# One level of Strassen in the down projection of a two-layer feed-forward, with weight splitting shared between two engines

## The chip, the core and the metric

The kernel runs on one core of a Trainium2 chip. Its engines each have their own instruction queue: TensorE (PE in the profile; its weight loads are PEld), VectorE (DVE), ScalarE (ACT), GpSimd (POOL) and SyncE (SP, which here issues DMA). The metric is the time of one execution in device microseconds (us), the median of several runs. All tensors are float32. The matmuls work on "fp32r" operands: a float32 number is split into a high part (a cast) and a low part (the number minus its high part), and a product is three matmuls, high x high, high x low and low x high, accumulated in PSUM.

## What is computed

A trunk of two layers on 512 tokens of width 1024: a recurrent mixer (layer 0) and stick-breaking attention (layer 1), each followed by a SwiGLU feed-forward of width 2816. The change lies in the feed-forward, whose reference is, per layer,

```
h = _rmsnorm(x, norm_ffn_g[layer])
x = x + (silu(h @ w_gate) * (h @ w_up)) @ w_down
```

with x 512 x 1024, w_gate and w_up 1024 x 2816 and w_down 2816 x 1024.

## The kernel before, in words

**Order of stages.** `run` (L1102) does the recurrent mixer, feed-forward 0, attention, feed-forward 1. The residual x is kept transposed in SBUF as eight tiles of 128 features x 512 tokens (`self.x`, L286).

**Units.** `ffn` (L611) walks over the 2816 hidden columns in six units (u = 0 to 5): five of 512 columns and a last one of 256. The gate and up products of a unit are already one 2 x 2 Strassen-Winograd step with seven products instead of eight (`product(q, ...)`, L632, q = 1 to 7). The stationary operands of these products are sums and differences of activations, prepared once per layer in `ffn_in` (L331); the moving operands are weight combinations. One product of a full unit is two chunks of 12 matmuls, 512 columns wide; of the last unit, one chunk of 24 matmuls, 256 wide. The products are collected in three pairs of PSUM banks that rotate from unit to unit (L679). `gate1` (L691) and the end of product 4 (L733 to L738) apply silu and the multiplication; the result is token-major, in the tiles `u2` and `hx`.

**Down.** The down projection of unit u-1 is woven into unit u. `turn` (L646) transposes two of the four 128-column blocks at a time on TensorE into banks 6 and 7 and splits them into high and low parts (`hh`). `down_pair` (L670) takes one weight chunk and makes two of the eight output tiles: 4 k tiles x 3 matmuls of 512 columns each, weights stationary, then one DVE add from PSUM onto x (L668). Four such pairs complete a full unit. Behind the loop (L741 to L782) follow the last pair or two of unit 4 and the half unit 5, into banks held open.

**Order.** In `ffn`, TensorE's instructions stay in program order (`manual_schedule`, L614); the other engines are ordered by a scheduler with priorities.

**Weights.** `plan` (L155) lists all weight chunks (128 x 1024, 512 KB) in order of use: 99 per feed-forward layer. `chunk` (L254) loads up to eight chunks ahead through SP's queue, and splits up to three ahead in the feed-forward: `Piece.source` (L74) first makes a Strassen combination on DVE where the product needs one (L76, 128 x 1024), then `split_piece` (L235) casts the high part on ACT (L236) and subtracts for the low part (L237) on the engine that `wl_engine` (L247) names. In a feed-forward the low parts of gate/up weights go to DVE and those of down weights to POOL. Outside, odd-numbered chunks go to POOL and even ones to DVE, except where listed. Four pairs of tiles take the split weights (three in one pool, `wh4`/`wl4` beside it, L223); with them the cast of a chunk waits until the matmuls four chunks back are done. Raw weights that are used once have four buffers (`raw_buf`), two quarters of each gate/up block have their own, doubled (`b1`, `b3`), and the running combination has two (`tt`).

**Norm.** For each x tile a square is added into `acc`, in `ffn_in` on POOL (L366, L380). In u = 0, between products 3 and 7, `norm_rs1` (L394) turns that into the tokens' scale with small matmuls and a chain of small DVE and ACT operations (L385 to L390).

**Slots.** Most 128 x 512 tiles come from an arena of 43 slots that lives throughout (NS1, x among them), and a second of 30 that exists only in the mixers (NS2).

Of the kernel before, what the change touches and what calls it, by code (L numbers as in the profile page):

```python
# [16 lines left out]
P = 128  # L17
# [12 lines left out]
NS1 = 43  # L30
NS2 = 30
FB = 512
NU = 5
# [11 lines left out]
class Unit:  # L45
    def __init__(self, kern, l, u):
        self.kern, self.u = kern, u
        self.w = FB if u < NU else FB // 2
        self.np = 2 if u < NU else 1
        self.kt = 2 if u < NU else 4  # L50
        self.src = kern.a["w_gu"][l, 8 * u:8 * u + 4 * self.np]
        self.b = {}


class Piece:
# [18 lines left out]
    def source(self):  # L74
# [20 lines left out]
        return b("t")  # L95


class Kern:
# [56 lines left out]
    def plan(self):  # L155
# [13 lines left out]
        def ffn(l):  # L169
            down = a["w_dn"][l]  # L170
            r = [self.unit(l, 0)]
            for u in range(1, NU + 1):
                p = self.unit(l, u)
                d = [[down[4 * (u - 1) + i]] for i in range(4)]
                h = len(p) // 7
                if u == 1:
                    order = (0, 1, 2, 3, d[0], 4, d[1], 5, d[2], 6, d[3])
                elif u < NU:
                    order = (0, 1, d[0], 2, 3, d[1], 4, d[2], 5, 6, d[3])
                else:  # L180
                    order = (0, 1, d[0], 2, 3, d[1], 4, 5, 6, d[2], d[3])
                r.append([e for q in order for e in (q if isinstance(q, list) else p[q * h:q * h + h])])
            r.append([down[20], down[21]])
            return [e for u in r for e in u]
# [17 lines left out]
    def unit(self, l, u):  # L202
        k = Unit(self, l, u)
        return [Piece(k, q, c) for q in ((1, 5, 6, 3, 7, 2, 4) if u else (1, 2, 5, 6, 3, 7, 4)) for c in range(k.np)]
# [78 lines left out]
    def setup(self):  # L283
        nc, a = self.nc, self.a
        c = self.const
        self.x = [self.new(f"x{k}") for k in range(KT)]  # L286
# [324 lines left out]
    def ffn(self, l, gnext):  # L611
        nc, tc = self.nc, self.tc
        mm = nc.tensor.matmul
        with tc.tile_pool(name=f"ffn{l}", bufs=1) as self.fp, tc.manual_schedule(engines={mybir.EngineType.PE}):  # L614
# [8 lines left out]
            tb = self.bank[6:]  # L623
            ab = [self.bank[2 * i:2 * i + 2] for i in range(3)]
# [3 lines left out]
            hh = [None] * 4  # L628
            hx = [self.new("hx", first=True) for _ in range(2)]
            rs = lambda t: self.rsT[:, t:t + 1]  # L630

            def product(q, unit, out, half, first=True):  # L632
# [13 lines left out]
            def turn(fs, banks, dst=None):  # L646
                for f, b in zip(fs, banks):
                    for t in range(NT):
                        nc.tensor.transpose(b[:, ts(t)], (u2 + hx)[t][:, ts(f)], self.ident)
                    h, lw = dst[f] if dst else (self.fp.tile([P, S], F32R, tag=f"{n}{f}", bufs=1,  # L650
                                                             name=f"{n}{f}_{self.used}") for n in ("hh", "hl"))
                    nc.scalar.copy(h, b)
                    nc.vector.tensor_tensor(lw, b, h.bitcast(F32), ALU.subtract)
                    if not dst:
                        hh[f] = (h, lw)

            def down(w, o, n, bank, first=True, last=True, cs=slice(0, S)):
                for k in range(n):
                    h, lw = hh[k]
                    ws = ts(o * n + k)  # L660
                    st, en = first and k == 0, last and k == n - 1
                    out = bank[:, :cs.stop - cs.start]
                    mm(out, lhsT=w[0][:, ws], rhs=h[:, cs], start=st, stop=False, skip_group_check=True)  # L663
                    mm(out, lhsT=w[0][:, ws], rhs=lw[:, cs], start=False, stop=False, skip_group_check=True)  # L664
                    mm(out, lhsT=w[1][:, ws], rhs=h[:, cs], start=False, stop=en, skip_group_check=True)  # L665

            def add(m, bank):
                nc.vector.tensor_tensor(self.x[m], self.x[m], bank, ALU.add)  # L668

            def down_pair(d):  # L670
                w = self.chunk()
                for i in range(2):
                    down(w, i, 4, tb[i])
                    add(2 * d + i, tb[i])

            for u in range(NU + 1):
                un = self.unit_of()
                w = un.w
                A, B, D = (ab[(u + i + l) % 3] for i in range(3))  # L679
                if u > 1:  # L680
                    turn((0, 1), tb)
                product(1, un, A, 0)
                for j in range(2):
                    nc.scalar.copy(r1[j][:, :w], A[j][:, :w])

                def second():
                    product(2, un, D, 0)
# [9 lines left out]
                if u == 0:  # L697
                    second()
                elif u > 1:
                    turn((2, 3), tb)  # L700
                product(5, un, B, 0)
                if u == 1:
                    turn((0, 1), tb)
                for j in range(2):
                    nc.scalar.copy(b5[j][:, :w], B[j][:, :w])
                if u > 1:
                    down_pair(0)
                product(6, un, A, 0, False)
                if u == 1:
                    turn((2, 3), tb)  # L710
# [469 lines left out]
```

## Time and profile before

| | |
|---|---|
| median of 3 runs | 1150.58 us (1150.24 to 1152.18) |
| span of the profiled execution | 1150.0 us |
| mean granted TensorE clock | 0.990 |
| feed-forward 0, from product 1 of u = 0 to attention's first matmul | 166.92 to 512.04 us |
| feed-forward 1, from product 1 of u = 0 | from 786.05 us |
| start of product 1 of u = 0 to 5, layer 0 | 166.92, 207.75, 270.74, 332.94, 395.15, 457.34 us |
| HBM read, written | 102.81 MB, 2.10 MB |

The profile is one execution with every instruction's start and duration. A line such as "L668 DVE ... x<-x,bank ... x87 | 59.6, 685 | 85.2 <-PE bank L665 84.3" is a group: source line, engine, operation, output from inputs, shapes, count; then its busy time in us and the mean of one in ns; then the engine's idle time just before these instructions and what ended most of it. In the timeline a row is start, duration, engine, line, operation and, in brackets, the idle time before it and its releaser. In the waits a row is who waited for whom: total us, number of times, longest. Matmuls overlap in their recorded durations, so their pace is read from one start to the next.

### The profile page before, as it was taken

How to read it: one execution, taken by the hardware profiler on the slowest of the kernel's cores; microseconds unless marked ns; L12 is line 12 of the kernel's file. 1: busy time of each engine (PE TensorE's matmuls, PEld its weight loads, DVE VectorE, ACT ScalarE, POOL GpSimd, SP SyncE). 2: the span in 40 equal slices, each digit the busy share in tenths (PEclk: the TensorE clock that was granted, in tenths of full speed). 3: DMA queues.
4: the chain of work that ended last, by engine and by line, in shares of the span. 5: the costliest groups of instructions: out<-in, count | busy, mean ns of one | idle time of the engine just before them, and what ended most of it. 6: DMA issues, size and time to landing. Idle time of an engine off the chain costs nothing. (4 is left out here: it accounts for less than half of the span.)

```text
span 1150.0 us, 14308 instructions
## 1 busy us (share of the span) xinstructions
PE 1120.0 (97%) x5363; PEld 931.0 (81%) x5363; DVE 816.6 (71%) x1080; ACT 647.0 (56%) x967; POOL 298.3 (26%) x167
## 2 busy tenths in 40 slices
PE   8999999999999999999999999899999999999995
PEld 6887788888888888988888888778788888888884
DVE  7878889767574757473488888679967575765655
ACT  6598576634353444453489999767544434343442
POOL 2451333020111111272054444314011111101231
PEclk9999999999999999999999999899999999999997
DMA  7222234332424222122434334033432331322201
GB/s 241 91 90 91 96 105 169 96 114 79 134 74 134 68 92 92 58 89 94 118 95 117 92 90 108 25 109 111 147 128 92 95 120 61 117 84 92 74 19 74
DMA packets 35862, 114.23 MB, mean 99 GB/s; under 512 B 4560, under 2 KB 5584, under 8 KB 35792
## 3 DMA queue, kind: packets, MB, share of 16 engines
q1 hardware_dynamic: 35504, 112.66, 30.9%
q8 instruction: 42, 0.69, 0.2%
q10 hardware_dynamic: 288, 0.66, 0.2%
q14 instruction: 28, 0.23, 0.1%
HBM read 102.81 MB, written 2.10 MB: 91 GB/s over the span
## 5 line engine op out<-in xcount | busy, mean ns | idle before, releaser
L237 POOL TENSOR_TENSOR wl<-raw,wh 128x1024 fp32r<-128x1024 f32 (+1 forms) x74 | 177.9, 2405 | 642.2 <-ACT wh L236 638.5
L236 ACT CAST wh<-raw 128x1024 fp32r<-128x1024 f32 (+1 forms) x154 | 155.9, 1016 | 186.1 <-PE bank L644 88.2
L642 PE MATMUL bank<-wh,ow 128*128 128x512 f32 (+1 forms) x480 | 179.4, 374 | 3.6 <-DVE st L389 3.6
L644 PE MATMUL bank<-wh,ow 128*128 128x512 f32 (+1 forms) x480 | 178.3, 372 | 0.0
L643 PE MATMUL bank<-wl,ow 128*128 128x512 f32 (+1 forms) x480 | 178.3, 371 | 0.0
L237 DVE TENSOR_TENSOR wl<-raw,wh 128x1024 fp32r<-128x1024 f32 (+1 forms) x80 | 98.5, 1234 | 46.0 <-ACT wh L236 45.1
L236 ACT CAST wh<-tt 128x1024 fp32r<-128x1024 f32 x66 | 69.4, 1052 | 109.5 <-PE bank L664 55.1
L663 PE MATMUL bank<-hh,wh 128*128 128x512 f32 (+1 forms) x324 | 125.4, 387 | 0.0
L664 PE MATMUL bank<-hl,wh 128*128 128x512 f32 (+1 forms) x324 | 125.3, 387 | 0.0
L665 PE MATMUL bank<-hh,wl 128*128 128x512 f32 (+1 forms) x324 | 125.2, 387 | 0.0
L668 DVE TENSOR_TENSOR x<-x,bank 128x512 f32<-128x512 f32 x87 | 59.6, 685 | 85.2 <-PE bank L665 84.3
L642 PEld LDWEIGHTS bank<-wh,ow 128*128 128x128 f32 x480 | 90.4, 188 | 19.7 <-ACT wh L236 4.4
L237 DVE TENSOR_TENSOR wl<-tt,wh 128x1024 fp32r<-128x1024 f32 x66 | 80.6, 1222 | 34.9 <-ACT wh L236 34.5
L270 PE MATMUL bank<-uh,wh 128*128 128x512 f32 x256 | 102.4, 400 | 1.8 <-ACT wh L236 1.2
L644 PEld LDWEIGHTS bank<-wh,ow 128*128 128x128 f32 x480 | 90.4, 188 | 15.7
L643 PEld LDWEIGHTS bank<-wl,ow 128*128 128x128 f32 x480 | 90.5, 188 | 15.3
L272 PE MATMUL bank<-uh,wl 128*128 128x512 f32 x256 | 100.3, 392 | 1.4 <-DVE wl L237 1.4
L271 PE MATMUL bank<-ul,wh 128*128 128x512 f32 x256 | 99.7, 390 | 0.3 <-DVE ul L326 0.3
L237 DVE TENSOR_TENSOR wl<-b,wh 128x1024 fp32r<-128x1024 f32 x44 | 54.8, 1246 | 51.8 <-ACT wh L236 51.6
L236 ACT CAST wh<-b 128x1024 fp32r<-128x1024 f32 x44 | 46.3, 1053 | 62.1 <-PE bank L644 26.7
L665 PEld LDWEIGHTS bank<-hh,wl 128*128 128x128 f32 x324 | 60.8, 188 | 12.4
L663 PEld LDWEIGHTS bank<-hh,wh 128*128 128x128 f32 x324 | 60.9, 188 | 12.1
(219 smaller groups left out, 2422.3 us busy)
## 6 DMA issues: line engine op xcount, KB each, us to landing
raw<-w_gu SPq DMA_DIRECT2D x44, 512.0 KB, 3.5
b<-w_gu SPq DMA_DIRECT2D x44, 512.0 KB, 3.9
raw<-w_dn SPq DMA_DIRECT2D x44, 512.0 KB, 3.5
raw<-w_qk SPq DMA_DIRECT2D x16, 512.0 KB, 3.4
raw<-w_in SPq DMA_DIRECT2D x14, 512.0 KB, 3.7
raw<-w_ao SPq DMA_DIRECT2D x8, 512.0 KB, 3.8
raw<-w_v SPq DMA_DIRECT2D x8, 512.0 KB, 3.5
qh<-qx SPq DMA_DIRECT2D x32, 128.0 KB, 2.4
```

The lines of the kernel that those rows point to most:

```text
L236: self.nc.scalar.copy(wh[:, c], raw[:, c])
L237: self.wl_engine(i).tensor_tensor(wl[:, c], raw[:, c], wh[:, c].bitcast(F32), ALU.subtract)
L270: mm(out, lhsT=wh, rhs=xh, start=first, stop=False)
L271: mm(out, lhsT=wh, rhs=xl, start=False, stop=False)
L272: mm(out, lhsT=wl, rhs=xh, start=False, stop=last)
L642: mm(out[j][:, :w], lhsT=oh[:, ts(j)], rhs=wh[:, ws], start=st, stop=False, skip_group_check=True)
L643: mm(out[j][:, :w], lhsT=oh[:, ts(j)], rhs=wl[:, ws], start=False, stop=False, skip_group_check=True)
L644: mm(out[j][:, :w], lhsT=ol[:, ts(j)], rhs=wh[:, ws], start=False, stop=en, skip_group_check=True)
L663: mm(out, lhsT=w[0][:, ws], rhs=h[:, cs], start=st, stop=False, skip_group_check=True)
L664: mm(out, lhsT=w[0][:, ws], rhs=lw[:, cs], start=False, stop=False, skip_group_check=True)
L665: mm(out, lhsT=w[1][:, ws], rhs=h[:, cs], start=False, stop=en, skip_group_check=True)
L668: nc.vector.tensor_tensor(self.x[m], self.x[m], bank, ALU.add)
```

## The change

- **Down projection.** For the five full units it becomes one Strassen-Winograd step, too: outputs in two halves of four tiles, tokens in two halves of 256, k in two halves of two tiles; seven products, `d1` to `d7`, each 4 output tiles x 2 k tiles x 3 matmuls of 256 columns, weights stationary. Each product takes a chunk of its own, so the plan has 7 in place of 4 (114 a layer instead of 99), from four loads as before. `DownPiece.source` makes the weight combinations on DVE: three of 128 x 1024 at d6, one at d5.
- **Activations.** The 16 transposes come in two turns, `t0` (blocks 0 and 2) and `t1` (1 and 3), both into banks 6 and 7. After each, `operands` makes one k tile of the seven moving operands: an ACT copy from PSUM, four subtractions on DVE, and four splits (cast on ACT, subtraction on DVE).
- **Banks.** Gate/up has two pairs of banks instead of three (`gb`), the down products have the pairs `db` and `tb` (banks 6 and 7, shared with the turns). Products accumulate on one another (d6, d7 and d4 on db; d3 on d5). After each product two DVE adds of 128 x 512 bring a pair of banks onto a half of four x tiles; for that x becomes one tile.
- **Order.** The steps of a unit are a written list (below). The result of the gate goes into `b5` in place (`hx` is gone), so the copy of product 5 into `b5` moves behind `t1`. The half unit's transposes (`tn`) lie between d3 and d4 of unit 4, and its down products follow all at once in the eight banks.
- **Low parts.** In a feed-forward POOL makes those of all down chunks, and of gate/up every second chunk (c = 1) in full units and the even products in the last unit; DVE the others.
- **Arenas.** NS1 43 to 30 (x no longer in it), NS2 30 to 40; the DMA scratch area is set to 1024.

```diff
     def wl_engine(self, i):
...
-            return self.nc.vector if isinstance(self.chunks[i], Piece) else self.nc.gpsimd
+            e = self.chunks[i]
+            dve = isinstance(e, Piece) and not isinstance(e, DownPiece) and (e.c == 0 if e.unit.np == 2 else e.q % 2)
+            return self.nc.vector if dve else self.nc.gpsimd
...
+class DownPiece(Piece):
+    LOADS = {1: (0,), 2: (1,), 6: (2, 3)}
...
+    def source(self):
+        un, kern, d = self.unit, self.unit.kern, self.unit.d
+        tt = lambda o, x, y, op=ALU.subtract: kern.nc.vector.tensor_tensor(o, x, y, op)
+        if self.q == 6:
...
+            tt(d["s1"], d[2], d[3], ALU.add)
+            tt(d["s2"], d["s1"], d[0])
+            tt(d[2], d[0], d[2])
+            return d["s2"]
+        if self.q == 5:
+            tt(d["s2"], d[1], d["s2"])
+            return d["s1"]
+        return d[{1: 0, 2: 1, 7: 2, 3: "s2", 4: 3}[self.q]]
...
+            def operands(p):
+                bx, by = tb
...
+                cx, ta, tc_ = (self.tmp() for _ in range(3))
+                nc.scalar.copy(cx, bx)
+                sub(ta[:, T0], cx[:, T1], cx[:, T0])
+                sub(ta[:, T1], by[:, T1], ta[:, T0])
+                sub(tc_[:, T0], by[:, T1], cx[:, T1])
+                split([t[:, p] for t in hop["a"]], cx[:, T0])
+                split([t[:, p] for t in hop["b"]], by)
+                sub(tc_[:, T1], by[:, T0], ta[:, T1])
+                for i, t in enumerate((ta, tc_)):
+                    split([o[:, p, 2 * i:2 * i + 2].rearrange("p a b -> p (a b)") for o in hop["t"]], t)
...
+            DOWN = {1: (db, True, (0, T0)), 2: (tb, True, (0, T0)), 6: (db, False, (0, T1)), 5: (tb, True, (1, T1)),
+                    7: (db, False, (1, T1)), 3: (tb, False, (0, T1)), 4: (db, False, (1, T0))}
+
+            def dproduct(q):
+                wh, wl = self.chunk()
+                banks, first, (i, cs) = DOWN[q]
+                for m in range(4):
+                    out = banks[m // 2][:, ts(m % 2, HS)]
+                    for p in range(2):
+                        h, lw = moving(q, p)
+                        ws = ts(4 * p + m)
+                        st = first and m % 2 == 0 and p == 0
+                        mm(out, lhsT=wh[:, ws], rhs=h, start=st, stop=False, skip_group_check=True)
+                        mm(out, lhsT=wh[:, ws], rhs=lw, start=False, stop=False, skip_group_check=True)
+                        mm(out, lhsT=wl[:, ws], rhs=h, start=False, stop=p == 1, skip_group_check=True)
+                for b in range(2):
+                    xs = self.xx[:, 4 * i + 2 * b:4 * i + 2 * b + 2, cs]
+                    nc.vector.tensor_tensor(xs, xs, banks[b].rearrange("p (m c) -> p m c", m=2), ALU.add)
...
+                A, B = gb[(u + l) % 2], gb[(u + l + 1) % 2]
+                D = db if u == 0 else B
...
+                def t0():
+                    turn((0, 2), tb)
+                    operands(0)
+
+                def t1():
+                    turn((1, 3), tb)
+                    g5_out()
+                    operands(1)
...
                 if u == 0:
+                    order = "g1 g2 g5 g6 g3 stats g7 gate1 g4"
+                elif u < NU:
+                    order = "g1 t0 g5 t1 g6 d1 g3 d2 d6 g7 d5 d7 g2 gate1 d3 d4 g4"
                 else:
+                    order = "g1 t0 g5 t1 g6 g3 d1 d2 d6 g7 d5 d7 g2 gate1 g4 d3 tn d4"
```

More of the change, by code (lines that the diff above doesn't have):

```diff
@@ L169, in ffn @@
         def ffn(l):
-            down = a["w_dn"][l]
-            r = [self.unit(l, 0)]
+            r = self.unit(l, 0)
             for u in range(1, NU + 1):
[L173 to L184, printed above, removed]
+                k, p = self.unit(l, u)
+                order = "g1 g5 g6 d1 g3 d2 d6 g7 d5 d7 g2 d3 d4 g4" if u < NU else "g1 g5 g6 g3 d1 d2 d6 g7 d5 d7 g2 g4 d3 d4"
+                r = r + [e for s in order.split() for e in (p[int(s[1])] if s[0] == "g" else [DownPiece(k, int(s[1]))])]
+            return r + [a["w_dn"][l, 20], a["w_dn"][l, 21]]
         full += ffn(0)
@@ L285, in setup @@
         c = self.const
-        self.x = [self.new(f"x{k}") for k in range(KT)]
+        self.xx = c.tile([P, KT, S], F32, name="x")
+        self.x = [self.xx[:, k] for k in range(KT)]
         self.u = [None] * KT
@@ L627, in ffn, with product @@
             r1, u2, b5 = ev
-            hh = [None] * 4
-            hx = [self.new("hx", first=True) for _ in range(2)]
             rs = lambda t: self.rsT[:, t:t + 1]
-            def product(q, unit, out, half, first=True):
+            T0, T1 = slice(0, HS), slice(HS, S)
+            hop = {}
+            def product(q, unit, out, first=True):
                 n, w = unit.np, unit.w
@@ L644, in product, with turn @@
                             mm(out[j][:, :w], lhsT=ol[:, ts(j)], rhs=wh[:, ws], start=False, stop=en, skip_group_check=True)
-            def turn(fs, banks, dst=None):
+            def turn(fs, banks):
                 for f, b in zip(fs, banks):
                     for t in range(NT):
[L649 to L674, printed above, removed]
+                        nc.tensor.transpose(b[:, ts(t)], (u2 + b5)[t][:, ts(f)], self.ident)
+            def ftile(n, shape):
+                return [self.fp.tile([P, *shape], F32R, tag=f"{n}{i}", bufs=1, name=f"{n}{i}_{self.used}")
+                        for i in "hl"]
@@ new lines, in down @@
+            def down(w, o, bank, cs=slice(0, S)):
+                out = bank[:, :cs.stop - cs.start]
+                for k in range(2):
+                    h, lw = (t[:, k, cs] for t in hop["n"])
+                    ws = ts(o * 2 + k)
+                    mm(out, lhsT=w[0][:, ws], rhs=h, start=k == 0, stop=False, skip_group_check=True)
+                    mm(out, lhsT=w[0][:, ws], rhs=lw, start=False, stop=False, skip_group_check=True)
+                    mm(out, lhsT=w[1][:, ws], rhs=h, start=False, stop=k == 1, skip_group_check=True)
@@ L678, in ffn, with g1, g2 @@
                 w = un.w
[L679 to L687, printed above, removed]
+                A, B = gb[(u + l) % 2], gb[(u + l + 1) % 2]
+                D = db if u == 0 else B
+                def g1():
+                    product(1, un, A)
+                    for j in range(2):
+                        nc.scalar.copy(r1[j][:, :w], A[j][:, :w])
+                def g2():
+                    product(2, un, D)
                     for j in range(2):
@@ new lines, in g5_out, with g6, g3 @@
+                def g5_out():
+                    for j in range(2):
+                        nc.scalar.copy(b5[j][:, :w], B[j][:, :w])
+                def g6():
+                    product(6, un, A, False)
+                    for j in range(2):
+                        nc.scalar.copy(u2[j][:, :w], A[j][:, :w])
+                def g3():
+                    product(3, un, B, False)
+                    for j in range(2):
+                        nc.vector.tensor_tensor(u2[j][:, :w], u2[j][:, :w], B[j][:, :w], ALU.add)
@@ L741, in ffn @@
+                for s in order.split():
+                    steps[s]()
             self.rel(*self.held)
```

148 lines of the change are left out of this document (73 added, 75 removed).

## The prediction

> **What bounds the kernel now.** I read the page first, then the busy times of the engines by stretch (cut where product 1 of a feed-forward unit begins), then TensorE's waits and its timeline.
>
> ```profile
> span 1150.0 us, 14308 instructions
> PE 1120.0 (97%) x5363; PEld 931.0 (81%) x5363; DVE 816.6 (71%) x1080; ACT 647.0 (56%) x967; POOL 298.3 (26%) x167
> ```
>
> ```profile
> core 0: us, PE busy (x) PEld busy (x) DVE busy (x) ACT busy (x) POOL busy (x), PEclk, DMA share, GB/s
> 332.94:395.15 62.21, 61.87 (x284) 51.19 (x282) 41.23 (x45) 26.73 (x33) 10.25 (x4) 1.00 0.31 102
> 166.92:207.75 40.83, 39.29 (x178) 32.35 (x176) 39.78 (x49) 27.57 (x36) 11.06 (x2) 1.00 0.53 181
> ```
>
> ```profile
> PE bank L642 <- DVE st L389: 3.6, 2, 2.1
> PE bank L649 <- DVE x L668: 2.8, 8, 0.3
> ```
>
> The second fence shows a steady unit (u = 3 of layer 0, 62.21 us) and u = 0 of layer 0. In the steady unit TensorE (PE) is busy for all but 0.3 us and DVE is free a third of the time; DMA runs at 0.31. In u = 0 DVE has nothing left: 39.78 of 40.83 us. TensorE's losses in the units are 3.6 us in two waits of u = 0, and 2.8 / 8 = 0.35 us at a transpose in each of eight units. So work taken from TensorE shortens the kernel, unless DVE, POOL or a wait takes its place. Recorded durations of matmuls overlap, so I take the pace from starts:
>
> ```profile
> 282.62 0.39 PE L663 MATMUL bank<-hh,wh 128*128 128x512 f32 x1
> ...
> 288.06 0.39 PE L642 MATMUL bank<-wh,ow 128*128 128x512 f32 x1
> ```
>
> ```profile
> 480.73 0.28 PE L642 MATMUL bank<-wh,s 128*128 128x256 f32 x1
> ...
> 489.36 0.40 PE L663 MATMUL bank<-hh,wh 128*128 128x512 f32 x1
> ```
>
> Between the first two lie the 24 matmuls of one down pair: 5.44 / 24 = 0.2267 us each at 512 columns. Between the second two lie three products of unit 5, 72 matmuls of 256 columns: 8.63 / 72 = 0.1199 us, a little over half.
>
> **The part removed from TensorE.** A full unit's down projection is 4 pairs x 24 = 96 matmuls of 512 columns: 21.76 us. Strassen makes it 7 products x 4 row tiles x 2 k tiles x 3 passes = 168 of 256 columns: 20.14 us. An eighth of the columns goes, but the narrow pace takes back part: 1.62 us a unit remain, and 16.2 us over the ten full units (five per layer). The gate/up products, the 16 transposes a unit and the last half unit's 48 matmuls stay the same in number. This is the whole direct gain, 1.4% of the span.
>
> **What is added beside it, for a steady unit.** Durations of single operations:
>
> ```profile
> L76 DVE TENSOR_TENSOR b<-b,b 128x1024 f32<-128x1024 f32 x22 | 26.6, 1217 | 0.2
> L668 DVE TENSOR_TENSOR x<-x,bank 128x512 f32<-128x512 f32 x87 | 59.6, 685 | 85.2 <-PE bank L665 84.3
> L334 DVE TENSOR_TENSOR t<-t,t 128x256 f32<-128x256 f32 x16 | 6.7, 420 | 0.2
> L653 DVE TENSOR_TENSOR hl<-bank,hh 128x512 fp32r<-128x512 f32 x40 | 25.6, 682 | 0.0
> L652 ACT CAST hh<-bank 128x512 fp32r<-128x512 f32 x40 | 22.2, 588 | 0.7
> L236 ACT CAST wh<-tt 128x1024 fp32r<-128x1024 f32 x66 | 69.4, 1052 | 109.5 <-PE bank L664 55.1 <-PE bank L644 32.4 <-issue 13.7
> L237 DVE TENSOR_TENSOR wl<-tt,wh 128x1024 fp32r<-128x1024 f32 x66 | 80.6, 1222 | 34.9 <-ACT wh L236 34.5
> 300.27 2.40 POOL L237 TENSOR_TENSOR wl<-raw,wh 128x1024 fp32r<-128x1024 f32 x1 [5.77 <-ACT wh L236]
> 301.86 0.69 DVE L668 TENSOR_TENSOR x<-x,bank 128x512 f32<-128x512 f32 x1 [1.93 <-PE bank L665]
> ```
>
> ACT: three more weight casts (3 x 1.05), and per round of operands one copy and four casts of 256 or 512 columns (ten in all, none above the 0.59 of 512 columns) for four casts that go: at most +6.7 us, 33.4 of 60. It is no bound. DMA: the same 512 KB pieces, 20 a layer as before, each asked for some six chunks ahead.
>
> DVE: 7 low parts leave (-8.5), 4 weight combinations come (+4.9), 14 adds of 0.69 replace 8 (+4.1), and the split of the turned activations (4 x 0.68) becomes two rounds of five 256-column and three 512-column operations, 5 x 0.42 + 3 x 0.68 = 4.1 us a round (+5.5). 41.2 + 6.0 = 47.2 us of some 60: 79%. POOL: 14 low parts of 2.40 instead of 4: 33.6 us, 56%. Neither engine is full by itself. But they are not independent:
>
> ```profile
> 254.39 2.41 POOL L237 TENSOR_TENSOR wl<-raw,wh 128x1024 fp32r<-128x1024 f32 x1 [8.48 <-ACT wh L236]
> 254.72 3.15 DVE L76 TENSOR_TENSOR tt<-b,raw 128x1024 f32<-128x1024 f32 x1
> 504.69 1.10 DVE L326 SCALAR_TENSOR_TENSOR ul<-x,par,uh 128x512 fp32r<-128x512 f32 x1
> 505.20 2.85 POOL L237 TENSOR_TENSOR wl<-raw,wh 128x1024 fp32r<-128x1024 f32 x1
> 177.26 9.76 POOL L380 TENSOR_TENSOR acc<-acc,t 128x512 f32<-128x512 f32 x1 [7.86 <-ACT t L378]
> 184.65 1.22 DVE L237 TENSOR_TENSOR wl<-b,wh 128x1024 fp32r<-128x1024 f32 x1
> 185.79 0.68 DVE L689 TENSOR_TENSOR r<-r,bank 128x512 f32<-128x512 f32 x1
> ```
>
> A DVE operation with both inputs in SBUF stands still while POOL works: the one that starts at 254.72 ends at 257.87, 1.07 us after POOL's, at 256.80. POOL stands still in its turn: its low part of 505.20 ends 2.26 us after DVE's end at 505.79. An add out of PSUM (301.86, inside POOL's 300.27 to 302.67) loses nothing. So the two share something that one holds at a time, and what counts is the sum of POOL's low parts and DVE's two-SBUF operations. In a steady unit after the change: 14 POOL low parts; on DVE 7 low parts, 8 gate/up and 4 down combinations of 1024 columns, 4 gate multiplies of 512 (taken at 0.68), and 4 in each operand round (two of 256, two of 512). Freed of waiting time, by the rows just read (2.26 and 1.07; 0.55 and 0.28 for 512 and 256 columns, in proportion): 31.6 + 20.3 + 2.2 + 3.3 = 57.5 us. At full recorded durations: 33.6 + 23.2 + 2.7 + 4.4 = 63.9 us. TensorE needs 62.21 - 1.62 - 0.35 = 60.2. The shared port is thus at 95 to 106%; before it was at 4 x 2.40 + 22 x 1.22 + 4 x 0.68, about 39 of 62. I take it as just holding, because the low bound comes from the rows in which both engines press, and each chunk may be late: four pairs of weight tiles let a cast start when the chunk four places back is done, so three chunks of 12 x 0.2267 = 2.72 us lie ahead of its use, less 1.05 and 2.40: 4.7 us of slack.
>
> **The wait that is added.** The two turns now share banks 6 and 7 with the operand round between them: turn 1 may not write until round 0 has read both banks. Queued behind it on TensorE is everything (program order). Its cover is product 5, 24 x 0.2267 = 5.44 us. Round 0 up to its last PSUM read is one ACT copy (0.59) and six DVE operations, two of which touch the port: 0.59 + 5 x 0.42 + 0.68 = 3.4 us. Free of POOL it is hidden; with one POOL low part in the way it takes 5.8, 0.4 late; with two 8.2, 2.8 late. No row shows this wait, so these are its bounds; a gain is excluded, since nothing is removed there, apart from the 0.35 us wait on L668, which goes because the add before it now has a whole product 4 to finish. POOL has two low parts to do near product 5 (the second chunk of product 6, and d1), so one in the way is likeliest and two are possible; I take 0.8 us for eight units: 6.4. In unit 5 the cover is 24 x 0.1199 = 2.88 us: 0.5 late without POOL, 2.9 with one low part; I take the middle, 1.7, twice: 3.4.
>
> **Unit 0.** It gains no products, but half its low parts go to POOL: 39.78 - 7 x 1.22 + 7 x 2.40 = 48.0 us, less six adds from PSUM (4.1) 43.9, against 40.83. DVE is relieved, which could end the wait of 1.5 to 2.1 us on L389 (DVE's queue held the add that product 4 waits for); POOL may come late. How late, the row at 177.26 says: POOL waited through eight microseconds of back-to-back DVE work, up to the first PSUM add at 185.79. 9.76 less the operation's own 1.30 is 8.5; less 4.7 of slack, 3.8. Ends: -1.8 and +3.8 a layer; I take +1.5, since DVE's queue is shorter after the change: +3.0 in all.
>
> On this row the Trainium skill would give less: "SBUF — State Buffer", section "Who interferes with whom", says that the second of the two blocks until the first has finished, which would be one DVE operation. By that rule POOL's low part waits 1.2 us, the slack covers it, and unit 0 adds nothing: 3.0 us off the sum. The measured 9.76 decides, so I keep the +1.5.
>
> **Edits with little in them.** x in one tile changes no operation but the adds already counted. The arenas: attention gets 70 slots instead of 65 beside x, and its rows show no wait for a slot. The plan grows by 15 chunks a layer (99 to 114), so attention's alternation of low parts between DVE and POOL swaps; I take 0, with 3 us either way (one 2.40 less 1.22 late at each of two or three places). The last half unit turns behind product d3 and hides behind d4 (2.88 us against 0.59 + 0.68 and the transposes): 0, or 1 us a layer lost.
>
> **Sum** against the profiled execution (span 1150.0; the median of 1150.58 is 0.6 longer): -16.2 - 2.8 + 6.4 + 3.4 + 3.0 = -6.2, so 1144.4 by the median.
>
> **Rivals.**
>
> *All hidden.* The port works at its 57.5 us, round 0 always misses POOL, u = 0 is relieved: -16.2 - 2.8 + 1.0 (unit 5 at 0.5), and 0 to 3.6 less in u = 0: 1129 to 1133, say 1132. For it: the 4.7 us of slack at every low part; against it: POOL is at work more than half of the time, and every round 0 would have to miss it.
>
> *The port takes TensorE's place (slower).* Two POOL runs fall on round 0, because a waiting DVE lets POOL's next run in: 2.8 us at eight turns. Unit: 60.2 + 2.8 = 63.0, 0.8 more than now, 6.4 us; unit 5: (2.9 - 1.62) x 2 = 2.6; u = 0 at 2 to 3.8 each, 4 to 7.6: +13 to +17, say 1165; with the port at its 63.9 us a unit instead, 8 x 1.7 + 2.6 + 7.6 = 24: 1174. It decides where waits come to more than 62.2 - 60.2 = 2.0 us a unit. For it: the 95 to 106%, and DVE's ordered queue, in which adds for banks stand behind blocked operations. Against it: those adds have 8 us until their bank is wanted (product 3 and d2 lie between d1 and d6), and whenever TensorE waits, the port catches up.
>
> *Weights do not load in time.* A narrow matmul has half the time to hide its load:
>
> ```profile
> L663 PEld LDWEIGHTS bank<-hh,wh 128*128 128x128 f32 x324 | 60.9, 188 | 12.1
> ```
>
> If 188 ns were the least that a matmul with a new weight can take, 168 (the page counts one load per matmul) would take 31.6 us, 9.8 more than now, 98 in all: 1249. The 72 matmuls at 0.1199, each with its load, speak against it. The Trainium skill, "TensorE: Matmul & The Clock Gate", section "The mechanism" of Part 3, states that a load overlaps running matmuls only in other row groups, which would forbid this overlap of full-height loads; the trace does not bear it out.
>
> **How the numbers follow.** A measurement of this kernel tells 0.2% (2.3 us) from no change. Forecast, 0.42: its own range 1140 to 1150, of which 0.31 is faster and 0.11 same. All hidden, 0.19: faster. The port as the bound, 0.36: 1149 to 1174, of which 0.05 is same and 0.31 slower. Late loads 0.01 and what I have not seen 0.02: slower. So faster 0.50, same 0.16, slower 0.34. The range leaves out the lower half of the hidden case (0.1), the top of the slower one (0.07) and the last (0.03): 1132 to 1167.
>
> **What would show it.** Down matmuls 128x256, 1680 or so, 0.12 us apart in the timeline: else the first term is wrong. In TensorE's waits a row for the transposes behind DVE's operand subtractions of 3 to 10 us in all: over 20 is the slower rival, none the hidden one. POOL near 550 us busy (298 and 106 low parts of 2.40 more); DVE's 1024-column rows with a mean well over 1.3 us where the port presses; a steady unit of 61.0 us. Waits on low parts (PE behind POOL) would be the slack of 4.7 us used up, which I hold to be zero in steady units.

## The result, and the profile after

The changed kernel takes 1250.91 us (median of 4 runs, 1248.97 to 1251.72) against 1150.59 (1150.24 to 1152.18): 1.0869 times as long, 95% interval 1.0854 to 1.0885. The prediction, 1144.4 with a range of 1132 to 1167, was wrong by about 106 us.

The page of the kernel after, its head, busy times and clock row:

```profile
span 1247.2 us, 16266 instructions
PE 1136.5 (91%) x6071; PEld 969.2 (78%) x6071; DVE 992.3 (80%) x1234; ACT 705.2 (57%) x1057; POOL 591.6 (47%) x271
PEclk9999998999999999999999999899899899989997
```

TensorE fell from 97% to 91%, so it waits; POOL doubled (591.6 for 298.3); no engine's busy share is above 91%. The stages, by the starts of product 1 in TensorE's timeline (us; u5 is taken up to attention's first matmul in layer 0, up to the end of the span in layer 1):

| | u0, u0 | u1, u1 | u2 to u4, each | u5 |
|---|---|---|---|---|
| before | 40.8, 41.4 | 63.0, 63.0 | 62.2 | 54.7, 72.9 |
| after | 56.6, 57.2 | 66.6, 66.6 | 68.6 to 68.9 | 65.5, 82.3 |

The loss is 31.6 in the two u0, 7.2 in u1, some 38.6 in the six steady units and 20.2 in u5: 97.6 together, close to the 97.2 by which the span grew. Attention is the same within 0.3. Nothing is won back in any unit.

Busy time by stretch, kernel after: the steady unit u3 and u0 of layer 0.

```profile
358.58:427.17 68.59, 62.44 (x354) 54.56 (x352) 56.75 (x61) 32.46 (x41) 41.19 (x14) 0.98 0.29 93
166.77:223.40 56.63, 42.94 (x177) 33.46 (x176) 53.27 (x49) 28.07 (x36) 23.52 (x9) 0.91 0.42 149
```

In u3, DVE is busy for 56.75 us where 47.2 were forecast, and POOL for 41.19 where 33.6 were: both are stretched. What TensorE waits for, whole kernel:

```profile
PE bank L679 <- DVE b L795: 26.7, 16, 4.7
PE bank L679 <- DVE t L685: 23.9, 10, 4.6
PE bank L672 <- DVE st L419: 18.0, 2, 9.0
PE bank L673 <- DVE wl L264: 6.1, 4, 1.7
...
PE bank L728 <- DVE x L733: 5.0, 2, 2.5
PE bank L729 <- DVE hal L685: 4.9, 5, 1.0
```

Nearly all of it is DVE's: turn 0 waits for the gate multiply (L795), turn 1 for the subtractions of round 0 (L685, the added wait), product 4 of u = 0 behind the norm's chain (L419). That DVE is held up rather than given more work shows in one group, the Strassen combinations that both kernels have 22 times (before: 1217 ns each). Kernel after:

```profile
L77 DVE TENSOR_TENSOR b<-b,b 128x1024 f32<-128x1024 f32 x22 | 46.2, 2099 | 0.0
```

The same instruction on the same tiles takes 2099 ns. How one such delay reaches TensorE is seen in the timeline of u3, DVE and POOL around turn 0:

```profile
359.91 2.71 POOL L264 TENSOR_TENSOR wl<-tt,wh 128x1024 fp32r<-128x1024 f32 x1 [2.95 <-ACT wh L263]
369.66 6.25 POOL L264 TENSOR_TENSOR wl<-tt,wh 128x1024 fp32r<-128x1024 f32 x1 [7.04 <-ACT wh L263]
```

```profile
360.30 3.41 DVE L77 TENSOR_TENSOR b<-b,b 128x1024 f32<-128x1024 f32 x1
363.63 1.21 DVE L264 TENSOR_TENSOR wl<-tt,wh 128x1024 fp32r<-128x1024 f32 x1
364.77 0.74 DVE L795 SCALAR_TENSOR_TENSOR b<-b,rsT,t 128x512 f32<-128x512 f32 x1
...
366.56 0.74 DVE L795 SCALAR_TENSOR_TENSOR b<-b,rsT,t 128x512 f32<-128x512 f32 x1
...
372.90 0.41 DVE L685 TENSOR_TENSOR t<-t 128x256 f32<-128x256 f32 x1
374.24 2.75 DVE L77 TENSOR_TENSOR tt<-raw,tt 128x1024 f32<-128x1024 f32 x1
376.92 0.68 DVE L685 TENSOR_TENSOR hbl<-bank,hbh 128x512 fp32r<-128x512 f32 x1
377.52 0.41 DVE L685 TENSOR_TENSOR t<-bank,t 128x256 f32<-128x256 f32 x1
```

A combination that starts while POOL works (360.30) ends 2.2 us late, and the two gate multiplies behind it come late for turn 0. Round 0 (L685) then stands behind five more wide operations of DVE, 367.23 to 372.99, none of them stretched. Then the reverse: POOL's low part of 369.66 takes 6.25 us, because DVE has one wide operation after another in its queue; where a gap lets POOL in, the next combination (374.24) takes 2.75, and behind it stands the last bank read of round 0 (377.52), for which turn 1 waits. TensorE, kernel after, at the same place:

```profile
365.56 0.33 PE L679 MATMUL bank<-ident,b 128*128 128x128 f32 x1 [1.16 <-DVE b L795]
367.36 0.48 PE L679 MATMUL bank<-ident,b 128*128 128x128 f32 x1 [1.47 <-DVE b L795]
...
369.34 0.63 PE L674 MATMUL bank<-wh,ow 128*128 128x512 f32 x1
369.77 0.63 PE L672 MATMUL bank<-wh,ow 128*128 128x512 f32 x1
...
371.20 0.39 PE L674 MATMUL bank<-wh,ow 128*128 128x512 f32 x1
371.43 0.39 PE L672 MATMUL bank<-wh,ow 128*128 128x512 f32 x1
```

After the two waits, matmuls of 512 columns start 0.43 us apart, twice the usual 0.23, until about 370.5; product 5 takes 6.49 us, where the undisturbed one of run e1 below takes 5.54. In u3 the waits add up to 6.15 us (1.16, 1.47, 2.55 at turn 1, 0.97 at d1). The unit is 8.5 longer than the 60.1 that TensorE needs (e1), so 2.3 are not waits: 1.8 of them lie in turn 0 and product 5, in the slow stretch.

### The profile page after: what moved, and what is told of

It is laid out like the page before. It is cut to its first block, busy times and chain, and to the rows that moved or that the text cites. A ratio compares the mean times of both kernels' runs of the same rounds, so it can differ in the third digit from the quotient of the medians.

```text
span 1247.2 us, 16266 instructions
## 1 busy us (share of the span) xinstructions
PE 1136.5 (91%) x6071; PEld 969.2 (78%) x6071; DVE 992.3 (80%) x1234; ACT 705.2 (57%) x1057; POOL 591.6 (47%) x271
## 4 chain that ended last, share of the span: by engine, by line
PE 45%; DVE 34%; issue 6%; ACT 5%; POOL 1%; DMA 1%; DVEq 0%; ACTq 0%; POOLq 0%
DVE tt L77 7%; DVE wl L264 6%; PE bank L672 4%; PE bank L299 4%; PE bank L673 4%; PE bank L674 4%; PE bank L301 4%; PE bank L300 4%; PE bank L729 4%; PE bank L730 4%; PE bank L728 4%; DVE b L77 3%; PE bank L1030 2%; DVE ds L118 2%; ACT wh L263 2%
## 5 line engine op out<-in xcount | busy, mean ns | idle before, releaser
L263 ACT CAST wh<-raw 128x1024 fp32r<-128x1024 f32 (+1 forms) x134 | 134.8, 1010 | 114.3 <-PE bank L674 48.1
L264 POOL TENSOR_TENSOR wl<-tt,wh 128x1024 fp32r<-128x1024 f32 x34 | 120.8, 3554 | 160.6 <-ACT wh L263 157.7
L263 ACT CAST wh<-tt 128x1024 fp32r<-128x1024 f32 x66 | 69.5, 1052 | 128.3 <-DVE tt L77 63.9
L733 DVE TENSOR_TENSOR x<-x,bank 128x512 f32<-128x512 f32 x140 | 93.2, 681 | 41.0 <-PE bank L730 40.9
L264 DVE TENSOR_TENSOR wl<-raw,wh 128x1024 fp32r<-128x1024 f32 (+1 forms) x60 | 73.4, 1228 | 52.9 <-ACT wh L263 52.9
L728 PE MATMUL bank<-hth,wh 128*128 128x256 f32 x320 | 90.8, 284 | 5.0 <-DVE x L733 5.0
L730 PE MATMUL bank<-hth,wl 128*128 128x256 f32 x320 | 90.5, 283 | 0.0
L729 PE MATMUL bank<-htl,wh 128*128 128x256 f32 x320 | 90.5, 283 | 0.0
L264 POOL TENSOR_TENSOR wl<-b,wh 128x1024 fp32r<-128x1024 f32 x20 | 57.1, 2854 | 56.4 <-ACT wh L263 56.4
L264 POOL TENSOR_TENSOR wl<-ds,wh 128x1024 fp32r<-128x1024 f32 x30 | 74.4, 2482 | 17.2 <-ACT wh L263 16.5
L998 POOL TENSOR_TENSOR spl<-t,sph 128x512 fp32r<-128x512 f32 (+1 forms) x32 | 36.4, 1158 | 85.8 <-DVE sph L997 77.5
```

What stands on the lines that cost most here:

```text
L263: self.nc.scalar.copy(wh[:, c], raw[:, c])
L264: self.wl_engine(i).tensor_tensor(wl[:, c], raw[:, c], wh[:, c].bitcast(F32), ALU.subtract)
L728: mm(out, lhsT=wh[:, ws], rhs=h, start=st, stop=False, skip_group_check=True)
L729: mm(out, lhsT=wh[:, ws], rhs=lw, start=False, stop=False, skip_group_check=True)
L730: mm(out, lhsT=wl[:, ws], rhs=h, start=False, stop=p == 1, skip_group_check=True)
```

## The experiments

Theory P: POOL's low parts and DVE's operations with two inputs in SBUF exclude each other (the "port" is the thing that only one of them holds at a time), and this holds back what TensorE waits for. Rival Q: the weight sums, which the scheduler gives a high priority, stand in DVE's queue ahead of gate multiplies and operand rounds, whatever POOL does. Later a question inside P arose: what sets the price of a collision. Where nothing else is said, a run is the kernel after with the edit shown; ratios are to the kernel before on the same chip.

**e1: gate/up low parts all on DVE.**

```diff
-            dve = isinstance(e, Piece) and not isinstance(e, DownPiece) and (e.c == 0 if e.unit.np == 2 else e.q % 2)
+            dve = isinstance(e, Piece) and not isinstance(e, DownPiece)
```

> The changed kernel with all gate/up low parts back on DVE; POOL keeps the down chunks only. Theory P (the shared port: POOL's low parts hold back DVE's two-SBUF operations; the profile after shows 12.7 us of such waiting on DVE in a unit of 68.6) expects the port's demand to fall from 57.5 to about 49 us a unit, so steady units of 62 to 63 us, u = 0 near 42 instead of 57, about 1170 us in all. Theory Q (the weight sums, issued at high priority, stand in DVE's queue ahead of the gate multiply and the operand rounds, whatever POOL does) expects DVE's queue to be 8.5 us a unit longer: units of 68 us or more, u = 0 no better, 1245 to 1265 us.

Measured: 1170.48 us, 1.0165 times before (1.0135 to 1.0194). The total is P's number, but its parts are not, so there is luck in it: the steady units take 60.1 us for 62 to 63, the two u0 44.9 and 45.9 for 42, and u5 takes 65.3 and 84.4, still 11 us a layer above the kernel before. Steady unit u3 of e1, busy times by stretch:

```profile
336.61:396.72 60.11, 60.11 (x354) 53.33 (x352) 60.10 (x67) 32.36 (x41) 20.21 (x7) 1.00 0.34 106
```

TensorE is busy throughout and the unit takes 60.1 us, what the prediction held TensorE to need (60.2). DVE is busy for 60.10 of 60.11 us, more than in the kernel after, and nobody waits: a full DVE is not by itself the trouble. What is left of the loss lies in u0 and u5; u1, at 63.3, is 0.3 above the kernel before.

**e2: the kernel before, with the new rule for low parts only.**

```diff
-            return self.nc.vector if isinstance(self.chunks[i], Piece) else self.nc.gpsimd
+            e = self.chunks[i]
+            dve = isinstance(e, Piece) and (e.c == 0 if e.unit.np == 2 else e.q % 2)
+            return self.nc.vector if dve else self.nc.gpsimd
```

> The kernel before with nothing but the new rule for gate/up low parts (half on POOL). Theory P expects steady units to stay within 1 us of 62.2 (port 43 of 62 us) and u = 0 to grow as in the changed kernel, by some 15 us a layer: about 1180 us. Theory Q, in which the added sums and the operand rounds do the harm, expects next to nothing: 1148 to 1155 us.

Measured: 1190.05 us, 1.0335 (1.0305 to 1.0365). Without any Strassen in the down projection the rule alone costs 39 us. Its longest waits are of the same kind: u = 0's, behind the norm's chain, and the transposes', there behind the adds onto x:

```profile
PE bank L644 <- DVE st L391: 15.2, 2, 7.8
PE bank L651 <- DVE x L670: 10.3, 12, 1.2
```

The two u0 grew by 14.9 and 14.2 us, as P had it. But u2 and u3 grew by 2.2 to 3.6, where P, with the port at 43 of 62 us (47 with full durations), had held them within 1: a first sign against counting the port's total.

**e3: weight sums at ordinary priority.**

```diff
+        e = self.chunks[i]
+        raw = e.source() if isinstance(e, Piece) else self.raw.pop(i)
         with self.tc.high_priority(self.PRI):
-            e = self.chunks[i]
-            raw = e.source() if isinstance(e, Piece) else self.raw.pop(i)
```

> The changed kernel with the weight sums (gate/up and down) issued at normal priority; casts and low parts keep theirs. Theory Q expects TensorE's waits at the two turns (50.6 us) to go for the most part: units of 63 us, 1190 to 1205 us. Theory P: the port's demand is the same, so waits only change place: units of 67 to 70 us, 1235 to 1265 us.

Measured: 1248.39 us, 1.0841 (1.081 to 1.0873). The order changed, the time hardly did: Q falls.

**e4: POOL fills its low parts with zeros instead of computing them.** The kernel leaves out the low parts that POOL would make in the feed-forwards; instructions on the other engines stay.

```diff
-        self.wl_engine(i).tensor_tensor(wl[:, c], raw[:, c], wh[:, c].bitcast(F32), ALU.subtract)
+        eng = self.wl_engine(i)
+        if self.ring4 is not None and eng is self.nc.gpsimd:
+            eng.memset(wl[:, c].bitcast(F32), 0.0)
+        else:
+            eng.tensor_tensor(wl[:, c], raw[:, c], wh[:, c].bitcast(F32), ALU.subtract)
```

> The changed kernel in which POOL fills the low parts that it has to make in the feed-forwards with zeros, so it no longer reads SBUF (left out: the low part of those weights, the result is less exact). DVE's queue keeps its work. Theory P expects no DVE operation in a feed-forward to be held back: units of 61 to 62 us, u = 0 near 41, 1140 to 1155 us. Theory Q expects the sums ahead of the turns to cost the same: only the 12.7 us of waiting shrinks, units of 65 to 66 us, about 1210 us.

Measured: 1131.84 us, 0.9829 (0.9801 to 0.9858), 119 us less than after and below P's range, too. Steady unit u3, and the group of combinations, of e4:

```profile
327.31:387.42 60.11, 60.11 (x354) 53.34 (x352) 44.73 (x60) 32.48 (x41) 13.38 (x14) 1.00 0.33 106
```

```profile
L77 DVE TENSOR_TENSOR b<-b,b 128x1024 f32<-128x1024 f32 x22 | 26.7, 1216 | 0.0
```

With as many POOL instructions, none of which reads SBUF in the feed-forwards, the combinations are back at 1216 ns, the waits are gone, and the units are at 60.11. The Trainium skill ("SBUF — State Buffer", section "Who interferes with whom") says that a DVE instruction with two SBUF inputs contends with a GpSimd instruction that reads SBUF, not with one that only writes it. The trace agrees: 1216 ns beside writes, 2099 beside reads. A memset is also shorter (0.96 us for 2.40) and doesn't wait for ACT's cast, and this run doesn't part these; that POOL's length alone isn't the cause is shown by the stretched DVE rows.

**e5: turn 1 and round 1 in banks of their own (db)**, so that nothing waits for round 0's bank reads.

```diff
-                bx, by = tb
+                bx, by = (tb, db)[p]
...
-                    turn((1, 3), tb)
+                    turn((1, 3), db)
```

> The changed kernel with the second turn (t1) and its operand round in the banks of db (free there) instead of banks 6 and 7, so that t1 no longer waits for round 0 to read them. If that bank wait is a cause of its own (the step that the prediction priced), the 23.9 us of waits on L685 go, with what the halved clock behind them costs: 1215 to 1225 us. Theory P expects round 1 and d1 to wait for the same DVE work instead: at least two thirds of it comes back, 1235 to 1250 us.

Measured: 1271.11 us, 1.1032 (1.101 to 1.1054), slower than both theories had it. The wait went to the next user of the operands, product d1:

```profile
PE bank L729 <- DVE hal L685: 22.4, 6, 4.6
...
PE bank L728 <- DVE t L685: 9.8, 8, 3.2
```

The bank was not a cause of its own here; DVE's round is late, and TensorE meets it at one place or another.

**e6: u = 0's low parts on DVE, the rest as after.**

```diff
-            dve = isinstance(e, Piece) and not isinstance(e, DownPiece) and (e.c == 0 if e.unit.np == 2 else e.q % 2)
+            dve = isinstance(e, Piece) and not isinstance(e, DownPiece) and (e.unit.u == 0 or (e.c == 0 if e.unit.np == 2 else e.q % 2))
```

> The changed kernel with the low parts of unit 0 alone back on DVE. Theory P: unit 0 falls from 57 to some 45 us, as in the run with all gate/up low parts on DVE, and nothing else moves: 1250 less 24, 1222 to 1230 us. If unit 0 were slow for the new work beside it (the sums of d6 made in its tail), it stays above 53 us and the time above 1240.

Measured: 1229.83 us, 1.0674 (1.0653 to 1.0695). u = 0 fell from 57 to 46 us, in the range that P gave. The wait of product 4 behind the norm's chain fell from 18.0 us in two to 10.2. This wait in the kernel after, TensorE's row and then DVE's:

```profile
215.79 0.77 PE L672 MATMUL bank<-wh,ow 128*128 128x512 f32 x1 [8.98 <-DVE st L419]
```

```profile
208.12 4.46 DVE L77 TENSOR_TENSOR tt<-b,raw 128x1024 f32<-128x1024 f32 x2
212.50 0.15 DVE L416 TENSOR_SCALAR st<-bank 128x4 f32<-128x4 f32 x1
212.57 0.16 DVE L417 RECIPROCAL st<-st 128x4 f32<-128x4 f32 x1
212.65 1.19 DVE L77 TENSOR_TENSOR b<-b,b 128x1024 f32<-128x1024 f32 x1
213.76 1.21 DVE L264 TENSOR_TENSOR wl<-raw,wh 128x1024 fp32r<-128x1024 f32 x1
214.90 0.15 DVE L418 SCALAR_TENSOR_TENSOR st<-st 128x4 f32<-128x4 f32 x1
214.97 0.67 DVE L788 TENSOR_TENSOR b<-b,bank 128x512 f32<-128x512 f32 x1
215.57 0.15 DVE L419 TENSOR_TENSOR st<-st 128x4 f32<-128x4 f32 x1
```

Operations of 0.15 us stand in DVE's queue behind wide ones that POOL stretches (two combinations in 4.46 us, 2.0 more than two take), behind some of them stands the add of product 7 (L788) that reads the bank into which product 4 accumulates, and TensorE stands for 8.98. The chain itself feeds no matmul of product 4: the view names the last of the operations in time (L419).

**e7: e1 with turn 1 in db in all units, and another order of u = 5** that leaves more products between an operand round and its use.

```diff
-                bx, by = tb
+                bx, by = (tb, db)[p]
...
-                    turn((1, 3), tb)
+                    turn((1, 3), db)
...
-                    order = "g1 t0 g5 t1 g6 g3 d1 d2 d6 g7 d5 d7 g2 gate1 g4 d3 tn d4"
+                    order = "g1 t0 g5 t1 g6 g3 g7 d1 g2 gate1 d2 d6 d5 g4 d7 d3 tn d4"
```

> All gate/up low parts on DVE, t1 in the banks of db, and in the last unit products 7, 2 and 4 moved ahead among the down products, so that more TensorE work lies between the turns and d1, d2, d6. In the run with the low parts on DVE the steady units stood at 60.1 us and the loss was 21 us in the turns and in the bank wait before d6 of the last unit (L733), 8 us in unit 0. Theory P with too little cover there expects most of the 21 us back, the halved clock with it: 1145 to 1155 us. If instead DVE as a whole is too full in the last unit, the waits move to other products: 1163 to 1170 us.

Measured: 1171.05 us, 1.0164 (1.0141 to 1.0186): a miss. u = 5 of layer 0 fell from 65.3 us to 58.2, but the steady units rose from 60.1 to between 62.7 and 64.3, with d1 now waiting for round 1 (16.9 us in 8 waits). Sharing banks 6 and 7 had been the better choice there.

**e8: e7 with the norm's chain in u = 0 at high priority.**

```diff
-                    self.norm_rs1(False)
+                    with tc.high_priority(200):
+                        self.norm_rs1(False)
```

> The kernel of the run before this one in the list, with the norm's chain of small DVE operations in unit 0 at high priority. If the 8.3 us that TensorE waits there (rsT and the silu behind it) come from the chain's place in DVE's queue, 6 to 9 us go: 1138 to 1148 us. If DVE has no room in unit 0 at all, the wait changes its name and stays: less than 2 us.

Measured: 1172.46 us, 1.0176 (1.0154 to 1.0197): nothing won. Product 4's wait is as long as before and is now put down to product 7's adds (L788, 8.3 us in two): the chain was moved ahead, the adds were not. In e10 below, with the adds and the first gate ahead, too, u0 falls from 45.7 to 40.2 us.

**e9: three gate/up low parts a unit on POOL** (c = 1 of products 1, 2 and 3 in units 1 to 4; none in u0 and u5).

```diff
-            dve = isinstance(e, Piece) and not isinstance(e, DownPiece) and (e.c == 0 if e.unit.np == 2 else e.q % 2)
+            dve = isinstance(e, Piece) and not isinstance(e, DownPiece) and (e.unit.u == 0 or e.unit.u == NU or e.c == 0 or e.q not in (1, 2, 3))
```

> The kernel after with fewer low parts on POOL: none of the first and the last unit, and three of the seven gate/up ones in units 1 to 4. Theory P (DVE and POOL share one port, and only what goes over its capacity costs time): without the seven moved parts the port needs some 49 us of a unit, three parts add 1.2 us each, 52.7 of 60, so units 2 to 4 stay at 60.1 to 61 us, and the kernel is near the one with all gate/up low parts on DVE: 1170 to 1178. Rival R (each low part on POOL holds DVE back by a fixed time, whatever else goes on): 3/7 of the 8.5 us, units of 63.7, some 3.6 x 8 = 29 us over 1170: 1196 to 1202.

Measured: 1201.35 us, 1.0445 (1.0425 to 1.0465), in the rival's range; the steady units take 64.6 us, 0.9 above the rival's 63.7. By the prediction's own low sum the port was at 53 of 60 us, by its high one at 59. So the sum over a unit didn't tell what the unit takes. More than half of the 4.5 us that u3 loses against e1 lies at a wait that the kernel after has in none of its steady units, product 7 for low parts made by DVE (waits; DVE and POOL in u3):

```profile
PE bank L673 <- DVE wl L264: 11.4, 12, 1.6
```

```profile
377.77 3.41 DVE L264 TENSOR_TENSOR wl<-b,wh 128x1024 fp32r<-128x1024 f32 x1
```

```profile
377.66 2.45 POOL L264 TENSOR_TENSOR wl<-ds,wh 128x1024 fp32r<-128x1024 f32 x1 [3.77 <-ACT wh L263]
```

POOL's operation here is a low part of the down projection, one of those that e1 has, too, without a wait. In e9's u3 product 7 takes 2.5 us more than in e1, d1 1.3 and turn 1 0.7.

**e12: the same with products 2, 4 and 7 instead.** In e9's unit u3 the subtraction that d1 waits for was blocked by the low part of product 3:

```profile
362.53 2.69 POOL L264 TENSOR_TENSOR wl<-b,wh 128x1024 fp32r<-128x1024 f32 x1 [3.31 <-ACT wh L263]
```

```profile
362.90 2.60 DVE L685 TENSOR_TENSOR hal<-t,hah 128x256 fp32r<-128x256 f32 x1
```

```diff
-e.q not in (1, 2, 3))
+e.q not in (2, 4, 7))
```

> The run with three gate/up low parts a unit on POOL, with another three: those of products 2, 4 and 7 in place of 1, 2 and 3, so that none of them is made while an operand round is in DVE's queue (there the profile showed the subtraction behind which product d1 waits blocked for 2.60 us by the low part of product 3). Theory L (a collision costs only where TensorE waits for the operation that is held up; the port's total of 53 of 60 us is not what decides): units 2 to 4 at 60.1 to 61.5, and 1170 to 1180. Rival R (a fixed price for each low part on POOL, wherever it lies): 64 to 65 a unit and 1195 to 1203.

Measured: 1204.24 us, 1.047 (1.0451 to 1.049); the steady units take 65.2, one of the six 63.6. Theory L, that another place would be free, falls too. The rows of e12 show another collision: the low part of product 4 takes the port at the end of each unit, here u3, while the two gate multiplies of `gate1` come up. POOL, then DVE:

```profile
393.71 3.01 POOL L264 TENSOR_TENSOR wl<-tt,wh 128x1024 fp32r<-128x1024 f32 x1 [3.20 <-ACT wh L263]
```

```profile
394.37 3.57 DVE L763 SCALAR_TENSOR_TENSOR u<-u,rsT,r 128x512 f32<-128x512 f32 x2
```

The pair takes 3.57 us instead of e1's 1.40, with DVE's queue behind it; at the end of u2 (329.20) it is the same. In u3 round 0 then begins 3.9 us after turn 0 instead of e1's 2.0, turn 1 waits 2.8 us, and product 6 after it takes 7.16 us instead of e1's 5.54. So u3 loses 3.1 us at turn 1, 1.6 in product 6 and 0.4 at turn 0, nearly all of its 5.1, and none of it where e9's u3 loses most. That the one leads to the other is read from the order of the queue; no run removes just this collision.

**e10: e1 with the left waits mended one by one.** Turn 1 in db in units 1 and 5 only, e7's order of u = 5, and in u = 0 the norm's chain, the adds of product 7 and the first gate at high priority. Below are the lines for turn 1 and for two of the priorities; the rest is as in e1 and e7.

```diff
-                bx, by = tb
+                bx, by = tb if p == 0 or 1 < u < NU else db
...
-                    turn((1, 3), tb)
+                    turn((1, 3), tb if 1 < u < NU else db)
...
-                    steps[s]()
+                    with tc.high_priority(200) if u == 0 and s in ("stats", "gate1") else ExitStack():
+                        steps[s]()
```

> All gate/up low parts on DVE, turn 1 in its own banks in units 1 and 5 only, unit 5 with its operand rounds further from their use, and in unit 0 the statistics, the adds of product 7 and the first gate ahead of the low parts. Theory P with the remaining waits as a second, smaller cause: units 2 to 4 back at 60.1, unit 1 at 61 to 62, unit 5 at 58, unit 0 at 42 to 45: 1143 to 1153, about the kernel before or a little under it. Rival (DVE's queue is full in unit 0 and what is taken from one wait returns in the next): unit 0 stays at 45 to 46 and the run ends at 1153 to 1162.

Measured: 1145.34 us (1143.51 to 1145.96), 0.9952 times before (0.9934 to 0.9971): a little faster than both kernels. u0 takes 40.2 and 40.5 us, lower than expected, the steady units 60.1; u1 was a miss at 64.2 (two waits of d1 for round 1).

**e11: e10 with the down projection's weight sums at ordinary priority.**

The edit is that of e3, for the down projection's chunks alone.

> As the kernel with the mended waits, and the weight sums of the down projection at ordinary priority, so that they stand behind the first unit's own work in DVE's queue. If DVE's load in unit 0 is what is left: unit 0 at 41 to 43, 1140 to 1150. If those sums cost nothing where they stood: within 2 us of the run with the mended waits.

Measured: 1145.74 us, 0.9941 (0.9918 to 0.9964), the same as e10 within the spread (1140.27 to 1146.87). Where they stood, those sums cost nothing that shows.

## Why the prediction was wrong, point by point

- **The direct gain was right.** The narrow matmuls keep their pace. TensorE's timeline of the kernel after, d2 and d6 in a steady unit:

```profile
393.51 0.28 PE L728 MATMUL bank<-hbh,wh 128*128 128x256 f32 x1
...
399.26 0.40 PE L672 MATMUL bank<-wh,s 128*128 128x512 f32 x1
```

  48 matmuls in 5.75 us are 0.1198 each, for 0.1199 forecast. With the port out of the way a unit takes 60.11 (e1, e4) for 60.2 forecast, and the all-hidden rival's 1132 is what e4 gives (1131.84). The late-loads rival named 1249, but this pace excludes it: the agreement with 1250.91 is a coincidence. (The section of the Trainium skill that the prediction cited there, "TensorE: Matmul & The Clock Gate", section "The mechanism", also allows a load into a background weight buffer; the prediction left that half out.)
- **The step that failed is the port: "I take it as just holding".** That the two engines exclude each other was read rightly from the rows at 254.72 and 505.20. But the 57.5 to 63.9 us of a 60.2 us unit were made into a question of capacity, with waits on low parts held at zero and waits on gate multiplies not in the sum. e2, e9 and e12 refute the frame itself: e2's port is at 47 of 62 us with full durations, and u2 and u3 lose 2.2 to 3.6; at 53 to 59 of 60 us e9's and e12's steady units lose 4.5 to 5.1, one 3.5. In its place the rows show lateness at single points: POOL's 2.4 us stand in front of one DVE operation, DVE's ordered queue moves back behind it, and TensorE stands at the next thing that it needs from there (6.15 us of waits in the kernel after's u3).
- **The added wait was mis-sized.** Turn 1 was taken at 0.8 us a unit, from nothing to 2.8; in u1 to u4 of layer 0 it is 4.6, 2.4, 2.5 and 1.1. The 3.4 us of round 0 up to its last PSUM read counted the round's own operations alone. DVE's wide ones stand before and between them: from ACT's copy on, the round takes 5.95 us to that point even in e1's u3, where nothing waits, and 7.97 in u3 of the kernel after. The larger part was not in the sum at all: turn 0 behind the gate multiplies (2.63 in u3, the longest 4.7 elsewhere), d1 (0.97), and the slow stretch after the waits (1.8 of the 2.3).
- **Unit 0 was held to +3.8 at most and lost 15.8.** The bound came from POOL's lateness; TensorE's waits on weights in layer 0's u0 are 4.6 us, not far from it, but by the view only 1.6 of them end with POOL's low parts and 3.0 with DVE's. What it missed is DVE's side. The step "DVE is relieved" counted seven low parts fewer, but DVE's remaining wide operations were stretched, and product 4's wait behind them and the norm's chain took 9.0 us in each layer where it had taken 1.5 and 2.1. The granted clock, 0.91 in u0, accounts for part of the rest.
- **Unit 5 was given 1.7 us a layer for turn 1 and lost 10.8 and 9.4.** Turn 1 was sized fairly: in layer 0 it waits 1.3. Not in the sum were turn 0 behind the gate multiplies (4.7) and d6 behind the adds of d1 (2.5). Taking the gate/up low parts off POOL doesn't bring this back, as all of it is left in e1; e4, in which POOL reads no low part, brings the two back to 55.6 and 72.8, and the order of e7 to 58.2 and 75.1.
- **The slower rival had the mechanism, not the price.** It said that waits behind L685 of over 20 us would mark it, and they are 23.9. It allowed 8 x 1.7 us in units 1 to 4 of both layers and 7.6 in u = 0; measured are 45.8 and 31.6. It, too, let each delay count once, at one wait.
- **Small terms.** POOL was to reach 550 us and is at 591.6, stretched as DVE is. Attention's swap of low parts came out at 0, as taken.

Shown: it is POOL's reading low parts that cost the time (e4: -119 us; e1: -80 for the seven gate/up ones; e2: +39 alone in the kernel before), and neither the priority of the sums (e3) nor the shared banks (e5). Not settled: what sets the price. That three gate/up low parts a unit cost 31 to 34 us whichever they are fits a fixed price for each, but the rows show none: e9 loses most in product 7, e12 at turn 1 and in the half-speed stretch behind it. Nor does stretched DVE work as such cost time: the combinations counted above take 1564 ns in e1, whose steady units lose nothing, and 1211 and 1215 in e9 and e12, whose units do. The rows show a chain through one late operation; no run here tests it alone, as DVE's order changes with each edit.

## What to carry to other kernels

When two engines exclude each other at a port, don't compare the sum of their work with the time available: list the operations of the one for which the bounding engine waits next, and price each at a full operation of the other in front of it, plus what follows from the wait. No run here tests this rule; it is read from the rows. Moving work to an idle engine is tried by itself first: here the half of the change that cost 39 us (e2) hid the half that, free of the port, is worth up to 20 (e4 against before). A written order with a full DVE can run without a wait (e1, e10), so a busy share says little about whether an engine is late.

## What the runs showed of the hardware

- The engine that is shut out can be shut out for longer than one operation of the other: POOL's 6.25 us at 369.66 lies beside three wide DVE operations and two narrow ones in a row (369.50 to 373.65), as the 9.76 at 177.26 lay beside several before.
- A wait on TensorE can cost more than itself. After 1.16 and 1.47 us with one transpose between them, in u3 of the kernel after, and in e12's u3 after 2.83, matmuls ran at half the pace for about 3 us; in u4, after the same two waits, for 6. After the 2.55 us at turn 1 of the same u3 they didn't (product 6 took 5.56, for 5.54 in e1), nor after 2.95 us at turn 1 of e1's u1. The granted clock (0.50 in these stretches of u3 and u4, kernel after):

```profile
366.96:370.37 3.41, 3.01 (x10) 2.62 (x11) 3.41 (x4) 3.17 (x5) 0.71 (x1) 0.50 0.02 5
435.22:442.05 6.83, 6.10 (x17) 5.04 (x18) 6.83 (x9) 3.95 (x6) 3.80 (x1) 0.50 0.00 0
```

  The Trainium skill ("TensorE: Matmul & The Clock Gate", section "What's actually happening") ties half speed to a free-running window of about 3.4 us that was idle. A free-running window fits that one wait halves the pace and another doesn't; here waits somewhat shorter than the window were enough.
